# Projection chunks moved into the first stage, and an output projection that is summed in PSUM by column blocks

## The chip, the cores and the metric

The kernel runs on one core of a Trainium2 chip. The metric is the device time of one execution in microseconds (us), as the median of several runs. A trace of one execution was taken with the hardware profiler. TensorE is called PE (its weight loads PEld), VectorE is DVE, ScalarE is ACT, GpSimd is POOL, and SyncE, which issues the large loads, is SP.

## What is computed

One layer of a transformer encoder over 256 tokens of width 2048, in f32, with modulation vectors computed from a condition vector `c`:

```python
mod = silu(c) @ mod_w + mod_b                       # 2048 -> 6 x 2048
sh_m, sc_m, g_m, sh_f, sc_f, g_f = split(mod, 6)
h = x * (1 + sc_m) + sh_m
q, k, v = split(h @ w_qkv + b_qkv)                  # 32 query heads, 8 key/value heads of 64
o = windowed_attention(rope(q), rope(k), v, sink)   # |q - k| <= 128, a sink logit per head
y = o @ w_o + b_o
x = layer_norm(alpha * x + (1 + g_m) * y)
h = x * (1 + sc_f) + sh_f
y = relu(h @ w1 + b1) ** 2 @ w2 + b2                # 2048 -> 8192 -> 2048
x = layer_norm(alpha * x + (1 + g_f) * y)
```

## The kernel before

**Weights.** All matrices come as chunks of 128 x 2048 f32 (1 MB), loaded by SP into five raw buffers, and three more in the first stage. To keep f32 accuracy, ACT casts each half of a chunk to a rounded high part (`wh`, lines 382 and 393), and DVE subtracts it from the raw half to get the low part (`wl`, line 351). Five high and five low halves may be ready ahead. A product is three matmuls (`mm3`, lines 685 to 687): high x high, high x low, low x high, each with 512 output columns. A chunk of the projection to queries, keys and values (24 chunks) or of the output projection (16) is 24 such matmuls; half a chunk is 12.

**The stream.** `S.plan` lists every chunk in the order of use. `S.pump` walks this list strictly in order: it issues loads while a buffer is free, casts and splits halves while there is room, and hands modulation chunks to their own step. `S.main` pumps until the next chunk has both halves ready, `S.done` after each half. `S.pace` is the number of modulation chunks that one call may take on the way.

**Modulation.** 96 chunks of `mod_w` are vector times matrix. A chunk is taken either by PE, with the condition vector as the weights (line 458, a "row" chunk), or by DVE, which multiplies the chunk with the broadcast vector and sums along each row (line 498, a "column" chunk). `MIXP` says for each of the 16 groups of the mixer whether PE takes it, `FFP` how many of the four columns of a feed-forward group go to PE, `GMP` how many blocks of the mixer's gate.

**First stage** (0 to about 143 us). `SEQ` is the order of loading: entry `n` is a chunk with four units (one k-tile of 128 rows times 512 columns) of three column blocks that are summed in six PSUM banks over all 16 k-tiles; entry `(g, p)` is a chunk with four k-tiles of another column block, whose two token tiles share one bank in turn, and each is added to SBUF when done (`quarter`, line 784); the list behind an entry names the modulation groups loaded after it. `first_order()` (line 80) writes out the order of the instructions of the three engines with a planner's costs and due times, and these are pinned. The other seven chunks of this projection are in `LATE`.

**Attention and output projection.** The loop from line 1121 runs 21 slots. Slots 0 to 15 each do the scores of half a head group and a token tile (line 922), the maximum on DVE (line 929), the exponential on ACT (line 939), and in the next slot the transposes (line 964) with their copies (line 966); the values (line 980) come every second slot and give `oT[j]` for one of four head groups `j`. Each slot also takes one whole chunk: LATE chunks up to slot 4, then output-projection chunks `(c, j)` (column block `c`, head group `j`) in the order of `OUTS`, all `c` for one `j` before the next. `project` (line 1034) takes two new PSUM banks for each chunk, and DVE then adds them to an SBUF tile `y` (lines 1075 and 1077); at `j == 2`, `project_0` (lines 1088, 1089) multiplies `y` by the gate and adds it to the scaled residual; at `j == 3`, `add_gated` (lines 989 to 991) adds the last part and gathers the statistics of the norm. The bias comes by a broadcast over all partitions. `SLOT_FILL` says how many modulation chunks are planned before each slot's chunk, first the gate's, then those of the feed-forward groups. The order on each engine is mostly program order; the framework's scheduler may move an instruction that is ready ahead of one that waits. After the loop come the norm, the first feed-forward matrix (from line 1221), and the rest.

## Time and profile before

| | |
|---|---|
| median of 3 runs | 1085.61 us (1085.3 to 1085.9) |
| span of the profiled execution | 1083.7 us, 1.9 us under that median |
| PE busy | 1064.7 us (98% of the span) |
| DVE busy | 785.3 us (72%) |
| ACT busy | 527.5 us (49%) |
| read from HBM | 289.57 MB |

The profiled execution has no time of its own beside its span; the 1.9 us that lie around the span are the difference to the median of the runs. Busy shares are averages over stages with different limits. Overlapping matmuls count as busy throughout, so PE's share says little of its gaps; the distance from the start of one matmul to the next says more.

### The profile page before, as it was taken

To read this page: it belongs to the slowest core of one execution; us is meant where nothing else is said; L and a number is where in the kernel's file an instruction comes from. 1 tells how busy PE (TensorE), PEld (TensorE's weight loads), DVE (VectorE), ACT (ScalarE), POOL (GpSimd) and SP (SyncE) were. 2 spreads that over 40 slices of the span, in tenths; PEclk is the share of its full clock that TensorE was granted. 3 is DMA by queue.
4 is the path that set the end of the run, shared out by engine and by line. 5 is a ranking of instruction groups with operands and counts; after the bars stand their busy time and mean duration, and the time that the engine had idled before them with its cause. 6 is when DMAs were issued, how large, how long until landed. Compare 5 with 4: busy or idle time off the path is not lost.

```text
span 1083.7 us, 16256 instructions
## 1 busy us (share of the span) xinstructions
PE 1064.7 (98%) x6519; PEld 881.5 (81%) x6519; DVE 785.3 (72%) x1134; ACT 527.5 (49%) x814; POOL 19.7 (2%) x41
## 2 busy tenths in 40 slices
PE   8999999999999999999999999999999999999997
PEld 6777776677777899988888888888888888888885
DVE  3587689798799888754688789656665557665795
ACT  2453348777772646633345443344553334554340
POOL 2000000000000000000000010000000000000000
PEclk9999999999999999999999999999999999999999
DMA  9999997898973997555777889756555555557522
GB/s 380 425 425 425 427 407 270 352 348 344 391 277 122 420 352 273 193 194 194 272 272 274 295 293 319 297 203 222 194 194 188 192 193 201 181 181 263 194 78 78
DMA packets 43692, 292.75 MB, mean 270 GB/s; under 512 B 4916, under 2 KB 5076, under 8 KB 9824
## 3 DMA queue, kind: packets, MB, share of 16 engines
q1 hardware_dynamic: 40256, 281.82, 69.3%
q0 software_dynamic: 2496, 8.43, 2.3%
q10 hardware_dynamic: 864, 1.45, 0.4%
q8 instruction: 51, 0.84, 0.3%
q14 instruction: 25, 0.20, 0.0%
HBM read 289.57 MB, written 2.11 MB: 269 GB/s over the span
## 4 chain that ended last, share of the span: by engine, by line
PE 91%; DVE 5%; DMA 1%; ACT 1%; issue 1%; SPq 0%; DVEq 0%; ACTq 0%
PE pa L685 17%; PE pa L687 17%; PE pa L686 16%; PE pa L1264 16%; PE pa L1266 8%; PE pa L1240 3%; PE pa L1238 3%; PE pa L1239 3%; DVE raw L498 2%; PE pm L458 2%; PE gv L458 1%; PE pa L922 1%; PE pt L964 1%; PE pa L980 1%; DMA raw<-in_mod 1%; DVE wl L351 1%
## 5 line engine op out<-in xcount | busy, mean ns | idle before, releaser
L351 DVE TENSOR_TENSOR wl<-raw,wh 128x1024 fp32r<-128x1024 f32 x332 | 403.7, 1222 | 222.4 <-ACT wh L382 205.6
L382 ACT CAST wh<-raw 128x1024 fp32r<-128x1024 f32 x298 | 311.6, 1052 | 346.3 <-PE pa L687 203.1
L685 PE MATMUL pa<-wh,g 128*128 128x512 f32 x816 | 324.1, 398 | 2.7 <-ACT g L782 1.4
L687 PE MATMUL pa<-wh,g 128*128 128x512 f32 x816 | 319.3, 391 | 0.5 <-DVE g L984 0.4
L686 PE MATMUL pa<-wl,g 128*128 128x512 f32 x816 | 319.0, 391 | 0.5 <-DVE wl L351 0.4
L1264 PE MATMUL pa<-g,wh 128*128 128x512 f32 x768 | 192.3, 392 | 0.0
L685 PEld LDWEIGHTS pa<-wh,g 128*128 128x128 f32 x816 | 153.3, 188 | 42.7 <-issue 8.2
L687 PEld LDWEIGHTS pa<-wh,g 128*128 128x128 f32 x816 | 153.3, 188 | 34.6 <-issue 1.3
L686 PEld LDWEIGHTS pa<-wl,g 128*128 128x128 f32 x816 | 153.5, 188 | 31.4 <-DVE wl L351 1.2
L1264 PEld LDWEIGHTS pa<-g,wh 128*128 128x128 f32 x768 | 138.3, 189 | 25.1 <-ACT wh L382 0.2
L498 DVE CUSTOM_DVE_ANT_0 raw<-raw,cb 128x2048 f32<-128x2048 f32 x52 | 118.5, 2283 | 9.3 <-ACT cb L868 5.6
L1266 PEld LDWEIGHTS pa<-g,wl 128*128 128x128 f32 x768 | 104.8, 190 | 7.5
L1266 PE MATMUL pa<-g,wl 128*128 128x256 f32 x768 | 107.1, 282 | 0.0
L1240 PE MATMUL pa<-g,wl 128*128 128x256 f32 x256 | 72.3, 284 | 1.9 <-DVE wl L351 1.9
L1238 PE MATMUL pa<-g,wh 128*128 128x256 f32 x256 | 72.7, 285 | 0.3 <-ACT g L1173 0.3
L1239 PE MATMUL pa<-g,wh 128*128 128x256 f32 x256 | 72.4, 284 | 0.0
L1240 PEld LDWEIGHTS pa<-g,wl 128*128 128x128 f32 x256 | 48.9, 192 | 2.1 <-DVE wl L351 2.1
L1238 PEld LDWEIGHTS pa<-g,wh 128*128 128x128 f32 x256 | 49.1, 192 | 1.0 <-ACT g L1173 0.6
L1239 PEld LDWEIGHTS pa<-g,wh 128*128 128x128 f32 x256 | 49.1, 192 | 0.4 <-issue 0.4
L393 ACT CAST wh<-raw 128x1024 fp32r<-128x1024 f32 x34 | 34.8, 1048 | 21.8 <-DMA raw<-in_wqkv 19.6
L939 ACT ACTIVATE g<-g,nm 128x256 f32<-128x256 f32 x64 | 31.8, 498 | 13.1 <-DVE nm L929 13.0
L929 DVE CUSTOM_DVE_ANT_0 g<-pa,msk,nsnk 128x256 f32<-128x256 f32 x64 | 27.1, 477 | 6.3 <-PE pa L922 6.3
(204 smaller groups left out, 743.6 us busy)
## 6 DMA issues: line engine op xcount, KB each, us to landing
raw<-in_mod SPq DMA_DIRECT2D x96, 1024.0 KB, 8.8
raw<-in_w SPq DMA_DIRECT2D x64, 1024.0 KB, 4.8
raw<-in_w1b SPq DMA_DIRECT2D x48, 1024.0 KB, 4.8
raw<-in_wqkv SPq DMA_DIRECT2D x24, 1024.0 KB, 15.3
raw<-in_wo SPq DMA_DIRECT2D x16, 1024.0 KB, 7.4
raw<-in_w1a SPq DMA_DIRECT2D x16, 1024.0 KB, 7.4
g<-in_x SPq DMA_DIRECT2D x4, 512.0 KB, 9.1
gb<-in_lnrow POOLq DMA_DIRECT2D x8, 256.0 KB, 5.7
```

The lines of the kernel that those rows point to most:

```text
L351: self.pinned(nc.vector.tensor_sub(l, r, f32(self.hs[n])))
L382: self.last[n] = nc.scalar.copy(h, s)
L393: self.pinned(nc.scalar.copy(h, s))
L498: S.pinned(nc.vector.tensor_tensor_reduce(out=raw, in0=raw, in1=cb, scale=1.0, scalar=0.0, op0=OP.mult, op1=OP.add, accum_out=self.dst))
L685: S.pinned(nc.tensor.matmul(ps, xh, wh, start=start, stop=False))
L686: nc.tensor.matmul(ps, xh, wl, start=False, stop=False)
L687: S.prev = nc.tensor.matmul(ps, xl, wh, start=False, stop=stop).ins
L1238: nc.tensor.matmul(o, wh(w, 128), hh, start=new, stop=False)
L1239: nc.tensor.matmul(o, wh(w, 128), hl, start=False, stop=False)
L1240: nc.tensor.matmul(o, wl(w, 128), hh, start=False, stop=end)
L1264: nc.tensor.matmul(ps, wh(k, 128), ff_in(k), start=k == 0, stop=False)
L1266: nc.tensor.matmul(ps[:, :256], wl(k, 128), ff_in(k)[:, :256], start=False, stop=k == NK - 1)
```

## The change

In the first stage, four more chunks of the projection are taken as quarters, 21 of 24 in all, in a new order (`SEQ`), and `LATE` shrinks to three. DVE takes seven mixer groups instead of six, and all of feed-forward groups 0 and 1; PE takes 12 chunks of the mixer's gate instead of 8, in three blocks of 512 columns instead of one of 1024.

The output projection sums a column block in two PSUM banks over all four head groups, with the bias added by a matmul (from a row loaded in slot 2 and split in slot 3), so that nothing is added on DVE until the block is whole; then `add_gated` also scales the residual. `OUTS` alternates column blocks 0 and 1 beside the attention and takes blocks 2 and 3 after it. `HALVES` says how many halves of a chunk each slot takes, starting with the two chunks ahead of slot 0: slots 0 and 1 one half, 2 to 4 none (they pump twice), 5 to 16 one, 17 to 26 two. There are 27 slots, the pace is 1 in them, and the gate is spread in slot 15 instead of 11.

```diff
-OUT_AT = 5
-X_AT = 11
-SLOT_FILL = (1, 1, 1, 1, 1, 1, 1, 2, 2, 2, 2, 2, 2, 2, 2, 2, 2, 2, 2, 2, 1, 0, 0)
+HALVES = (2, 2, 1, 1, 0, 0, 0, 1, 1, 1, 1, 1, 1, 1, 1, 1, 1, 1, 1, 2, 2, 2, 2, 2, 2, 2, 2, 2, 2)
+X_AT = 12
+SLOT_FILL = (2, 2, 2, 3, 3, 3, 1, 0, 0, 1, 0, 0, 1, 0, 0, 1, 0, 0, 1, 2, 2, 2, 2, 2, 2, 1, 1, 0, 0)
 MIXG = (1,) * 16
-MIXP = tuple(int(k not in (4, 6, 8, 10, 12, 14)) for k in range(16))
+MIXP = tuple(int(k not in (6, 7, 9, 11, 12, 13, 15)) for k in range(16))
 FFG = (4, 4, 4, 4)
-FFP = (2, 2, 4, 0)
-GMP = 1
+FFP = (0, 0, 4, 0)
+GMP = 3
...
-        out += [("rg" + which, h, i, 0) for h in range(p) for i in range(8)]
-        out += [("cg" + which, 0, k, 0) for k in range(8 * p, NK)]
+        out += [("rg" + which, h, i, 0) for h in range(p) for i in range(4)]
+        out += [("cg" + which, 0, k, 0) for k in range(4 * p, NK)]
...
-SEQ = [(0, [1, 2]), (1, [3]), (2, []), ((0, 3), [4]), ((0, 4), [5]), (3, [6]), (4, [7]), (5, []), ((1, 3), [8]), ((1, 4), [9]), (6, [10]), (7, [11]), (8, [12]), ((2, 3), [13]), (9, [14]), (10, [15]), (11, [])]
+SEQ = [(0, []), (1, [1, 2, 3]), (2, []), ((0, 5), []), ((0, 3), []), (3, [4, 5, 6]), ((0, 4), []), (4, [7]), ((1, 4), []), (5, []), ((1, 5), [8]), (6, [9]), ((1, 3), []), (7, [10, 11]), ((2, 5), []), (8, [12]), ((2, 3), []), (9, [13]), ((2, 4), [14]), (10, []), (11, [15])]
...
-        def add(ps, c):
-            nc.tensor.matmul(ps, sel[:, c * 128:c * 128 + 128], hl, start=False, stop=True)
+        def add(ps, c, stop=True):
+            nc.tensor.matmul(ps, sel[:, c * 128:c * 128 + 128], hl, start=False, stop=stop)
...
-                m = Mod([MODS["rg" + which, h, i, 0] for i in range(8)], 256)
+                m = Mod([MODS["rg" + which, h, i, 0] for i in range(4)], 128)
...
-            nc.scalar.copy(r, m.ps[:, :256])
-            for x in range(2):
-                nc.tensor.transpose(pt[:, x * 128:x * 128 + 128], r[:, x * 128:x * 128 + 128], ident)
-            v = pt[:, :256].rearrange("p (x j q) -> p j x q", x=2, j=4)[:, :, :, 0]
-            d = self.col[:, 8 * h:8 * h + 8].rearrange("p (j x) -> p j x", j=4)
-            b = self.gb[:, 8 * h:8 * h + 8].rearrange("p (j x) -> p j x", j=4)
+            nc.scalar.copy(r[:, :128], m.ps[:, :128])
+            nc.tensor.transpose(pt[:, :128], r[:, :128], ident)
+            v = pt[:, :128].rearrange("p (j q) -> p j q", j=4)[:, :, 0]
+            d, b = (u[:, 4 * h:4 * h + 4] for u in (self.col, self.gb))
             nc.vector.tensor_tensor(d, v, b, op=OP.add)
...
-    LATE = [(3, 3), (2, 4), (3, 4), (0, 5), (1, 5), (2, 5), (3, 5)]
+    LATE = [(3, 3), (3, 4), (3, 5)]
...
-    OUTS = [(c, j) for j in range(4) for c in range(4)]
-    for n in range(-PRE, OUT_AT + 16):
+    OUTS = [(0, 0), (1, 0), (0, 1), (1, 1), (0, 2), (1, 2), (0, 3), (1, 3), (2, 0), (2, 1), (2, 2), (2, 3), (3, 0), (3, 1), (3, 2), (3, 3)]
+    halves = taken = 0
+    for n in range(-PRE, len(HALVES) - PRE):
         plan_late(SLOT_FILL[n + PRE])
         if n == X_AT:
             S.side[len(S.q)] = lambda: load_rows()
-        if n + PRE < len(LATE):
-            wq(*LATE[n + PRE])
-        elif n >= OUT_AT:
-            S.plan(a["wo"][OUTS[n - OUT_AT]])
+        halves += HALVES[n + PRE]
+        while 2 * taken < halves:
+            v = (LATE + OUTS)[taken]
+            if taken < len(LATE):
+                wq(*v)
+            else:
+                S.plan(a["wo"][v])
+            taken += 1
...
-    BEGIN = [(3, 3), (2, 4), (0, 5)]
+    BEGIN = [(3, 3), (3, 4), (3, 5)]
...
-    def add_gated(ps, t, c, gt, stats):
+    def add_gated(ps, t, c, gt, stats, scale=None):
         tmp = sml.tile([128, 512], F32, name="tmp", tag="t2", bufs=3)
         z = part(xs, t, c)
         nc.vector.tensor_tensor(tmp, ps, gt(c), op=OP.mult)
-        nc.vector.tensor_add(z, z, tmp)
+        if scale is None:
+            nc.vector.tensor_add(z, z, tmp)
+        else:
+            nc.vector.scalar_tensor_tensor(z, z, scale, tmp, op0=OP.mult, op1=OP.add)
         nc.vector.bn_stats(stats[t][:, c], z)
...
+    out_of = {}
+
     def project(c, j):
 
-        pss = [bank() for _ in range(NT)]
...
-                mm3(pss[t], oh[:, s], ol[:, s], wh(r), wl(r), r == 0, r == 3)
+                mm3(pss[t], oh[:, s], ol[:, s], wh(r), wl(r), j == 0 and r == 0, j == 3 and r == 3)
...
+                add_gated(pss[t], t, c, g1, st, ALPHA)
...
         for r in (0, 2):
             for t in range(NT):
                 step(t, (r, r + 1))
+            if r and j == 0:
+                for t in range(NT):
+                    bo(pss[t], c, False)
             S.done()
             if r == 0:
                 yield
-        for t, ps in enumerate(pss):
-            if j == 0 and t == 0:
-                ys[c] = g4b()
-            y = part(ys, t, c)
-            if j == 0:
-                nc.vector.tensor_add(y, ps, bo(c))
-            elif j < 3:
-                nc.vector.tensor_add(y, y, ps)
-            else:
-                add_gated(ps, t, c, g1, st)
-        if j == 2:
-            project_0(c)
-
-
-    def project_0(c):
-
-        for t in range(NT):
-            y, z = part(ys, t, c), part(xs, t, c)
-            nc.vector.tensor_mul(y, y, g1(c))
-            nc.vector.scalar_tensor_tensor(z, z, ALPHA, y, op0=OP.mult, op1=OP.add)
+        if j == 3:
+            for t in range(NT):
+                add_gated(pss[t], t, c, g1, st, ALPHA)
...
+    def chain():
+        for v in LATE[PRE:]:
+            yield from qkv(*v)
+            yield
+        for v in OUTS:
+            yield from project(*v)
+            yield
+
     todo = []
+    work = chain()
     S.behind = True
-    for n in range(OUT_AT + 16):
+    S.pace = 1
+    for n in range(len(HALVES) - PRE):
...
+        k = HALVES[n + PRE]
...
-        next(w, None)
+        if k:
+            next(work)
+        else:
+            S.pump(2)
         for f in mid:
             f()
-        next(w, None)
+        if k > 1:
+            next(work)
         if 0 < n <= 16 and n % 2 == 0:
             todo.append(values(n - 1))
-        if n == 11:
+        if n == 2:
+            split_bo, bo = bias_rows(a["bo"], D)
+        if n == 3:
+            split_bo()
+        if n == 15:
             g1 = m_gm.spread([g4(), g4()])
             st = [sml.tile([128, 4, 6], F32, name=f"st{t}", bufs=2) for t in range(NT)]
-        if n == 17:
+        if n == 24:
             ff_columns(0)
+    S.pace = VECS
```

More of the change, by code (lines that the diff above doesn't have):

```diff
@@ L571, in __init__ @@
             for h in range(p):
-                m = Mod([MODS["rg" + which, h, i, 0] for i in range(8)], 256)
+                m = Mod([MODS["rg" + which, h, i, 0] for i in range(4)], 128)
                 m.out = lambda m=m, h=h: self.rows(m, h)
                 self.ms.append(m)
-                rows += [(m, i) for i in range(8)]
+                rows += [(m, i) for i in range(4)]
             self.col = cst.tile([128, NK], F32, name="col" + which)
             cols = [(Col(MODS["cg" + which, 0, k, 0], self.col[:, k:k + 1]), 0)
-                    for k in range(8 * p, NK)]
+                    for k in range(4 * p, NK)]
             self.set(rows, cols)
@@ L1032, in normed @@
             tc.keep_in_program_order(nc.vector.tensor_scalar(z, z, mv[:, 0:1], rstd, op0=OP.subtract, op1=OP.mult))
+    out_of = {}
     def project(c, j):
-        pss = [bank() for _ in range(NT)]
+        pss = out_of[c] = out_of.get(c) or banks()
         last = j == 3 and c == 3
```

12 lines of the change are left out of this document (2 added, 10 removed).

## The prediction, made before the change was run

> **What bounds the kernel now.** I read the page first, then the busy time by stage, then the groups of the attention stage, then single instructions. From the page: busy engines, granted clock, and the chain that ended last.
>
> ```profile
> PE 1064.7 (98%) x6519; PEld 881.5 (81%) x6519; DVE 785.3 (72%) x1134; ACT 527.5 (49%) x814; POOL 19.7 (2%) x41
> ...
> PEclk9999999999999999999999999999999999999999
> ...
> PE 91%; DVE 5%; DMA 1%; ACT 1%; issue 1%; SPq 0%; DVEq 0%; ACTq 0%
> ```
>
> PE carries 91% of the chain at a full clock: time is PE's work plus PE's gaps. Busy time by stretch (PE, PEld, DVE, ACT, POOL, clock, DMA share, GB/s):
>
> ```profile
> 0.00:143.50 143.50, 134.94 (x1129) 105.36 (x1129) 90.47 (x137) 55.83 (x79) 6.19 (x18) 0.99 1.00 417
> 143.50:165.00 21.50, 21.10 (x133) 15.25 (x131) 20.48 (x23) 8.81 (x13) 0.64 (x2) 1.00 0.86 358
> 165.00:325.50 160.50, 159.75 (x1162) 115.92 (x1161) 140.24 (x302) 122.33 (x297) 3.15 (x6) 1.00 0.88 335
> 325.50:349.50 24.00, 24.00 (x117) 19.06 (x117) 21.72 (x37) 4.96 (x6) 0.00 (x0) 1.00 0.36 128
> 349.50:405.00 55.50, 51.85 (x476) 48.13 (x476) 47.50 (x77) 32.86 (x49) 0.00 (x0) 1.00 0.95 369
> 405.00:1083.70 678.70, 673.09 (x3514) 577.74 (x3513) 464.89 (x562) 302.73 (x373) 9.74 (x16) 1.00 0.62 218
> ```
>
> These are the first stage, the way into the attention, the 16 attention slots, the end of the output projection, the start of the feed-forward, and the rest. The change ends at 349.5, so I keep the last two rows as they are. PE's busy time hides its gaps, since matmuls overlap; two neighbours from the timeline and four entries of the chain give the real price of one:
>
> ```profile
> 346.67 0.39 PE L685 MATMUL pa<-wh,g 128*128 128x512 f32 x1
> 346.89 0.39 PE L686 MATMUL pa<-wl,g 128*128 128x512 f32 x1
> 347.12 0.39 PE L687 MATMUL pa<-wh,g 128*128 128x512 f32 x1
> ```
> ```profile
> 131.39 1.01 PE gv L458 x32
> ...
> 188.87 1.88 PE pa L980 x16
> 190.74 1.06 PE pa L922 x8
> ...
> 224.31 1.02 PE pt L964 x8
> ```
>
> A matmul of 512 columns costs 0.227 us from start to start ((347.12-346.67)/2, with the rounding), so a weight chunk of 24 costs 5.45 and half a chunk 2.72. A modulation chunk on PE costs 1.01. An attention slot costs scores 1.06, transposes 1.02 and half of a values step of 1.88: 3.02. In 165 to 325.5 that is 16 x 3.02 = 48.3, three rounds of query transposes (8 of the L964 kind each) 3.1, and, by the two rows below, 131 x 3 matmuls = 89.2 and modulation 16.1: together 156.7 of 160.5, or 97.6%. PE's gaps there are 3.8.
>
> ```profile
> 165.00:325.50 160.50, 52.09 (x131) 24.58 (x131) 1.00 0.88 335
> ...
> 165.00:325.50 160.50, 16.13 (x368) 9.41 (x368) 1.00 0.88 335
> ```
>
> These are the same stretch for line 687 alone, then for line 458 alone.
>
> **PE's work.** Modulation moves from PE to DVE: the mixer's groups lose one (2 chunks), feed-forward groups 0 and 1 lose 4 each, the mixer's gate gains 4 (12 instead of 8): 6 fewer, -6.1 us. The output bias, until now added by DVE, becomes 8 matmuls of 512 columns: +1.8. Transposes for the gate rise by one and for the others fall by two: nothing. Sum **-4.2**.
>
> **First stage.** Four more weight chunks come here and leave the later stages: 4 x 5.45 = 21.8 us of PE, moved. This stage was 143.5 and becomes about 143.5+21.8-2.0 = 163.3. Its cover is data: up to 143.5 the queue moved 143.5 x 0.417 = 59.8 MB, while 49 loads and x are 53.5, so 4 more loads (4.2 MB, 10 us at that rate) arrive earlier than PE can use them. DVE has 90.5 there and gets 8 low halves, 2 columns and 6 evictions, priced from these rows:
>
> ```profile
> L351 DVE TENSOR_TENSOR wl<-raw,wh 128x1024 fp32r<-128x1024 f32 x35 | 42.5, 1219 | 20.1 <-ACT wh L393 15.1 <-ACT wh L382 5.0
> L498 DVE CUSTOM_DVE_ANT_0 raw<-raw,cb 128x2048 f32<-128x2048 f32 x12 | 27.2, 2284 | 5.6 <-ACT cb L868 5.6
> ...
> L784 DVE TENSOR_TENSOR g<-g,pa 128x512 f32<-128x512 f32 x6 | 4.1, 686 | 6.6 <-PE pa L687 6.5
> ...
> ACT wh L393 <- DMA raw<-in_wqkv: 18.6, 5, 4.4
> ```
>
> 8 x 1.22 + 2 x 2.28 + 6 x 0.69 = 18.5: 109 of 163, not a bound. The last row (waits, 27 to 143) says that the cast waited 18.6 us in sum for weights to land; the new order asks for weights ahead of several modulation pairs. PE is idle 8.6 (143.5-134.94) in this stage, a part of it before the first data, where nothing is altered. I take **-2**; bounds -4 (about half of that idle gone) and +3 (nine quarter chunks instead of five share one bank, each with an eviction of 0.69 that the next must await; other units cover it now).
>
> **Attention.** Up to now a slot carried a whole chunk, 5.45 of PE. Now slots 0 and 1 carry half each, 2 to 4 none, 5 to 15 half each, because only two column blocks may be open and each needs the head group just finished. DVE, the second-busiest, is relieved (groups of 165 to 325):
>
> ```profile
> L1077 DVE TENSOR_TENSOR g4b<-g4b,pa 128x512 f32<-128x512 f32 x15 | 10.2, 681 | 3.5 <-PE pa L687 3.5
> L1075 DVE TENSOR_TENSOR g4b<-pa,g4b 128x512 f32<-128x512 f32 x8 | 5.4, 685 | 1.7 <-PE pa L687 1.7
> ...
> L1088 DVE TENSOR_TENSOR g4b<-g4b,g 128x512 f32<-128x512 f32 x7 | 4.6, 682 | 0.0
> L1089 DVE SCALAR_TENSOR_TENSOR g<-g,g4b 128x512 f32<-128x512 f32 x6 | 3.9, 684 | 0.0
> ```
>
> These 24.1 us go. DVE was not the bound, so by themselves they bring nothing. ACT becomes the tightest (groups, then one slot in order of time):
>
> ```profile
> L382 ACT CAST wh<-raw 128x1024 fp32r<-128x1024 f32 x34 | 35.4, 1043 | 13.0 <-PE pa L687 12.7
> L939 ACT ACTIVATE g<-g,nm 128x256 f32<-128x256 f32 x64 | 31.8, 498 | 13.1 <-DVE nm L929 13.0
> L954 ACT ACTIVATE g<-g,rs 128x256 f32<-128x256 f32 x64 | 27.6, 501 | 5.5 <-DVE rs L951 5.2
> L966 ACT COPY g<-pt 128x512 f32<-128x512 f32 x32 | 17.1, 576 | 2.4 <-PE pt L964 2.4
> ```
> ```profile
> 234.70 0.19 ACT L941 ACTIVATE es<-es 128x4 f32<-128x4 f32 x1
> 234.94 1.04 ACT L382 CAST wh<-raw 128x1024 fp32r<-128x1024 f32 x1
> 235.89 1.71 ACT L954 ACTIVATE g<-g,rs 128x256 f32<-128x256 f32 x4
> ```
>
> Only the casts shrink with the chunks: 122.3-35.4 = 86.9 stays, and 13 halves (2 of the last projection chunk, 11 of the output projection) add 13.5: 100.4. PE has 48.3+3.1+13 x 2.72+9 gate chunks 9.1+4 bias matmuls 0.9 = 96.8. ACT is now the longer lane. If it reaches the 97.6% that PE reached, the stage takes 102.9, PE's gaps are 6.1 instead of 3.8, and this costs **+2.3**. Bounds: -3.8 (PE is fed from elsewhere and loses nothing) and +12.6, the slower case below.
>
> A rule speaks against thinner slots. The Trainium skill, TensorE: Matmul & The Clock Gate, section What's actually happening, says that TensorE falls to half its clock after an idle window of about 3.4 us. By it each such gap would cost another 1.7 us as an estimate. The trace agrees as far as it goes: the granted clock is 1.00 from 143.5 on, where PE's gaps are small, and below that only at the start, as the rival on the clock quotes.
>
> **After the attention.** Ten chunks follow, 20 x 2.72 = 54.4 of PE. DVE gets some 20 low halves (24.4), 10 to 12 columns (23 to 27) and 6 gated additions of three passes each:
>
> ```profile
> L989 DVE TENSOR_TENSOR tmp<-pa,g 128x512 f32<-128x512 f32 x7 | 4.8, 686 | 2.1 <-PE pa L687 2.0
> L991 DVE BATCH_NORM_STATS2 st<-g 128x6 f32<-128x512 f32 x7 | 4.7, 687 | 0.1
> L990 DVE TENSOR_TENSOR g<-g,tmp 128x512 f32<-128x512 f32 x7 | 4.7, 683 | 0.1
> ```
>
> 6 x 2.06 = 12.3, so 60 to 64 against 54.4. Five low halves made ahead are 13.6 us of PE's work and cover that debt; bounds 0 and +5, I take **+1**. The gate row is now spread after slot 15 and first used in slot 18. Its way through memory (timeline of POOL, then the DMA issues with their us to landing):
>
> ```profile
> 281.41 0.51 POOL L600 DMA_DIRECT2D rowm<-grow  x1 [12.74 <-ACT grow L599]
> 286.82 1.08 POOL L602 DMA_DIRECT2D g<-rowm  x2 [4.91 <-DMA rowm<-grow]
> ```
> ```profile
> g<-rowm POOLq DMA_DIRECT2D x2, 512.0 KB, 11.6
> ```
>
> From the write's issue at 281.41 to 286.82+11.6 = 298.4 are 17 us, against two to three slots of 5.5 to 8. It may come a little late; then DVE stands at the first gated addition with the low halves queued behind it, and the same five halves cover PE. Nothing taken. The new addition with a scale (0.684 at line 1089) costs what the plain one does (0.683 at line 990). Splitting the bias is a few operations in slots 2 and 3, where DVE has room, and the 1 MB of bias broadcast goes away.
>
> **Sum.** -4.2-2+2.3+1 = -2.9. The profiled span of 1083.7 becomes 1080.8; the median of the runs stands 1.9 above the span (1085.6-1083.7), so the forecast is **1082.7 us**.
>
> **Rivals.**
> *PE alone sets the pace.* The order of the instructions may let PE take halves early whenever ACT is behind. Then the gaps beside the attention are gone (-3.8), the first stage gains 3, and the tail costs nothing: 1085.6-4.2-3.8-3 = 1074.6; with a little lost, 1076. For it: PE reached 97.6% in the old stage. Against it: ACT's own lane of 100.4 is longer than PE's 96.8.
>
> *ACT's latency, slower.* In a slot with half a chunk nothing lies between the transposes and the values step, so PE stands until ACT has copied both transposed tiles, and scores follow only then. ACT per two slots: exponentials 2.2 (4 x 0.5 and 0.19), cast 0.95, copies 1.07, scaling 1.7, all twice, and one cast of the result 0.58: 12.4; and it stands about 1.5 in every second slot, since the values step and the next scores (1.88+1.06) outlast the scaling (1.7): 13.9 for two, 6.95 each. Without a chunk, 5.95 each. 11 x 6.95 + 5 x 5.95 = 106.2, the first output chunk has nothing made ahead (+2), and the way from scores 15 to values 15 is bare (+5): 113.2, gaps 16.4 instead of 3.8, +12.6. With nothing won in the first stage and 2.5 lost at the end: 1085.6-4.2+12.6+2.5 = 1096.5. It decides as soon as a slot takes over 6.7 us on average. For it: ACT waited 13.0 on DVE's maxima at line 939 even with slack. Against it: the scores of the next slot depend on none of this and can go first.
>
> *The clock falls.* At the start, where PE waits for the first data, the granted clock was lower (same columns as the stretches above):
>
> ```profile
> 0.00:27.00 27.00, 22.61 (x244) 16.33 (x244) 9.12 (x31) 6.57 (x11) 6.19 (x18) 0.94 0.94 380
> ```
>
> 0.06 x 27 = 1.6 us of PE's work lost. Were that to happen in slots 2 to 4 and once at the end of the attention, on top of the slower case: 1096.5+4 x 1.6 = 1103. Against it: gaps there should be under 2 us, and the old stage's gaps left the clock at 1.00. The skill's rule cited above is this mechanism.
>
> *It cancels.* Four banks held from slot 5 on leave four for scores (2), transposes and values; the moved work and the lost cover balance: 1085.6.
>
> **How the numbers follow.** Forecast case 0.50, its own range 1078 to 1090; PE alone 0.22; ACT's latency 0.22; the clock 0.02; cancelled 0.04. No change means within 0.2%, 2.2 us, about what a measurement can tell. Of the forecast's half, 0.22 lies below 1083.4, 0.17 within, 0.11 above. Faster 0.22+0.22 = 0.44, same 0.17+0.04 = 0.21, slower 0.11+0.24 = 0.35. The range 1073 to 1098 takes in the bounds of the attention term.
>
> **What will show it.** The last bias matmul of the first stage should end near 163, not before 143.5 as now; if it ends after 167, the first-stage step is wrong. From first scores to the last values step should be about 103; over 110 means the latency case, under 98 the first rival. ACT should be busy over 90% of that stretch. Tail matmuls should run 0.227 apart, else DVE's debt was not covered. Line 458 should show 38 chunks' worth (6 fewer) and line 498 58 columns. The forecast fails if slots 5 to 15 show PE waiting over 1 us each for line 966's copies or for casts, or if anything after 405 moves.

## The result, and the profile after

The changed kernel takes 1113.89 us (median of 4 runs, 1111.92 to 1116.54); the kernel before, beside it, 1085.76 us. The ratio is 1.0259, 95% interval 1.0241 to 1.0278: slower by 28 us, above the predicted range of 1073 to 1098. The profiled execution has a span of 1114.8 us against 1083.7. Every ratio here and below is of fast runs and leaves out one execution, the profiled one of the last kernel, which took 3724.6 us.

From the page of the kernel after: busy engines, and the granted clock in 40 slices.

```profile
PE 1076.5 (97%) x6460; PEld 890.0 (80%) x6460; DVE 782.6 (70%) x1116; ACT 528.7 (47%) x814; POOL 22.4 (2%) x45
...
PEclk9999999889999999999999999999999999999999
```

Every busy share is about what it was. Only the two eights in the clock's line say where to look. Busy time by stretch of the kernel after (PE, PEld, DVE, ACT, POOL, clock, DMA share, GB/s): first stage, way in, slots 0 to 4, slots 5 to 14, slot 15 to the last values, tail, start of the feed-forward, rest.

```profile
0.00:158.40 158.40, 151.90 (x1159) 120.89 (x1159) 110.85 (x159) 64.81 (x87) 6.21 (x18) 1.00 1.00 417
158.40:190.90 32.50, 25.20 (x330) 18.79 (x328) 24.62 (x30) 8.51 (x14) 1.14 (x2) 0.95 0.91 345
190.90:234.30 43.40, 30.01 (x259) 19.16 (x260) 34.41 (x81) 29.09 (x75) 3.68 (x6) 0.82 0.86 328
234.30:304.80 70.50, 70.43 (x382) 48.44 (x381) 56.48 (x151) 62.12 (x175) 0.00 (x0) 0.99 0.58 201
304.80:323.50 18.70, 18.70 (x95) 13.06 (x95) 13.27 (x26) 12.20 (x29) 1.63 (x3) 1.00 0.78 279
323.50:379.00 55.50, 53.81 (x259) 42.39 (x255) 31.57 (x39) 16.28 (x16) 0.00 (x0) 1.00 0.61 222
379.00:434.50 55.50, 51.85 (x470) 48.03 (x470) 47.08 (x73) 33.10 (x49) 0.00 (x0) 0.99 0.94 368
434.50:1114.80 680.30, 674.65 (x3519) 579.29 (x3517) 464.36 (x562) 302.65 (x373) 9.77 (x16) 1.00 0.62 218
```

The same columns of the kernel before, for slots 0 to 4 and 5 to 14 (cut at the first scores and at the scores of slots 5 and 15):

```profile
165.10:209.50 44.40, 44.13 (x285) 31.00 (x285) 36.06 (x82) 37.65 (x91) 0.40 (x1) 1.00 0.86 320
209.50:310.40 100.90, 100.43 (x792) 73.29 (x790) 89.77 (x193) 72.83 (x181) 2.64 (x5) 1.00 0.94 359
```

Slots 0 to 4 hold 24 matmuls on weights now, where they held 103, and four modulation chunks as before (128 narrow matmuls for 64 wide ones): almost half of PE's work there is gone. They take 43.4 us, where they took 44.4. To see this in each stage I count PE's instructions and price them from start to start as the prediction did: "work" is that sum, "gap" is the length less the work. For slots 0 to 4 of the kernel after these are the main groups (line, engine, operation, names, shapes and count, then busy time, mean ns and idle time before):

```profile
L983 PE MATMUL pa<-g,g 128*64 128x256 f32 x24 | 6.6, 571 | 0.0
L967 PE MATMUL pt<-ident,g 128*128 128x128 f32 x32 | 6.1, 320 | 2.7 <-ACT g L957 2.7
L925 PE MATMUL pa<-g,g 64*128 64x256 f32 x40 | 5.9, 412 | 0.2 <-ACT g L911 0.2
L458 PE MATMUL pm<-raw,cact 128*32 128x128 f32 x128 | 4.3, 276 | 0.0
L688 PE MATMUL pa<-wh,g 128*128 128x512 f32 x8 | 3.4, 420 | 0.0
```

24 x 1.88/16 + 32 x 1.02/8 + 40 x 1.06/8 + 128/32 x 1.01 + 3 x 8 x 0.227 = 21.7; with the query transposes and the bias matmuls 23.3. So 20.1 of 43.4 us are gap, and PE's 30 us of "busy" hold matmuls that took longer at the low clock (a matmul of line 983 took 571 ns on average here and 385 before). What the low clock adds is in the gap too.

| stage | before: length, gap | after: length, gap |
|---|---|---|
| first stage | 143.4, 18.4 | 158.4, 13.8 |
| way in | 21.7, 1.2 | 32.5, 10.1 |
| slots 0 to 4 | 44.4, 1.9 | 43.4, 20.1 |
| slots 5 to 14 | 100.9, 3.6 | 70.5, 10.1 |
| slot 15 to last values | 16.7, -0.1 | 18.7, 2.5 |
| tail | 22.0, 0.2 | 55.2, 2.7 |
| start of feed-forward | 56.0, 4.0 | 56.0, 4.7 |

Over the whole kernel work fell by 4.3 us, as predicted (4.2); by the table it is 5.2 in these stages, since a few matmuls more fall into the rest now (3519 against 3514). Gaps rose from 29.2 to 64.0, that is by 34.8, and 34.8-4.3 = 30.5 of the 31.1 us between the spans is told by that. Over half of the rise is in slots 0 to 4 (18.2), a quarter on the way in (8.9). PE's two longest waits in the kernel after between 158 and 240 (engine, tile and line, what it waited for: sum, times, longest):

```profile
PE pt L910 <- DVE rs L954: 10.3, 1, 10.3
...
PE pm L458 <- DMA raw<-in_mod: 6.2, 3, 3.7
```

The second is the way in: gate chunks that are not loaded yet stand in PE's line ahead of the query transposes. The first stands in slot 2; DVE's timeline there (start, length, engine, line, operation), then PE's:

```profile
203.69 2.15 DVE L889 TENSOR_TENSOR g<-g,trig 128x512 f32<-128x512 f32 x2
205.76 1.82 DVE L892 TENSOR_TENSOR g<-g,trig 128x512 f32<-128x512 f32 x2
...
209.32 1.22 DVE L351 TENSOR_TENSOR wl<-raw,wh 128x1024 fp32r<-128x1024 f32 x1
210.46 2.28 DVE L498 CUSTOM_DVE_ANT_0 raw<-raw,cb 128x2048 f32<-128x2048 f32 x1
...
212.67 3.49 DVE L351 TENSOR_TENSOR wl<-raw,wh 128x1024 fp32r<-128x1024 f32 x3
216.08 0.15 DVE L950 TENSOR_TENSOR rs<-sm,es 128x4 f32<-128x4 f32 x1
216.15 1.22 DVE L894 TENSOR_TENSOR g<-g,g 128x1024 f32<-128x1024 f32 x1
```
```profile
206.20 1.04 PE L967 MATMUL pt<-ident,g 128*128 128x128 f32 x8
217.51 1.94 PE L910 MATMUL pt<-ident,g 128*128 128x128 f32 x8 [10.28 <-DVE rs L954]
```

Four low halves and one column, 7.0 us in sum, are work for later chunks. They stand in DVE's line ahead of the softmax's small step (L950) and of the last addition of the rotary step (L894), for which the query transposes wait. PE has nothing else to do, since the slot has no chunk.

The gap of slots 5 to 14 is of another kind. The profile lists no wait of PE there. What grew is the scores (line 922 before, 925 after; groups of these slots, then PE's timeline in the kernel after):

```profile
L922 PE MATMUL pa<-g,g 64*128 64x256 f32 x82 | 11.8, 404 | 0.0
```
```profile
L925 PE MATMUL pa<-g,g 64*128 64x256 f32 x81 | 18.5, 421 | 0.0
```
```profile
280.63 1.13 PE L925 MATMUL pa<-g,g 64*128 64x256 f32 x8
281.69 0.50 PE L688 MATMUL pa<-wh,g 128*128 128x512 f32 x1
...
290.26 1.13 PE L925 MATMUL pa<-g,g 64*128 64x256 f32 x4
291.31 1.08 PE L983 MATMUL pa<-g,g 128*64 128x256 f32 x8
```

Eight score matmuls in one run hold PE for 1.06 us (281.69-280.63), the price used above; four alone hold it for 1.05, and the other four, after the values, for as long again. About as many matmuls are busy 6.7 us longer (18.5-11.8), and the gap of these slots rose by 6.5 (10.1-3.6). So here PE does not stand: the scores cost twice as much where the scheduler takes them apart. Why it does so is not shown.

### The profile page after: what moved, and what is told of

It reads as the page before. It is cut to its first block, busy times and chain, and to the rows that moved or that the text cites. A ratio compares the mean times of both kernels' runs of the same rounds, so it can differ in the third digit from the quotient of the medians.

```text
span 1114.8 us, 16139 instructions
## 1 busy us (share of the span) xinstructions
PE 1076.5 (97%) x6460; PEld 890.0 (80%) x6460; DVE 782.6 (70%) x1116; ACT 528.7 (47%) x814; POOL 22.4 (2%) x45
## 4 chain that ended last, share of the span: by engine, by line
PE 91%; DVE 4%; DMA 3%; ACT 1%; issue 1%; SPq 0%; DVEq 0%; ACTq 0%
PE pa L688 17%; PE pa L690 17%; PE pa L689 16%; PE pa L1271 16%; PE pa L1273 8%; PE pa L1245 3%; PE pa L1247 3%; PE pa L1246 3%; DMA raw<-in_mod 2%; PE pa L925 2%; PE pa L983 2%; PE gv L458 1%; PE pt L967 1%; PE pm L458 1%; DVE raw L498 1%
## 5 line engine op out<-in xcount | busy, mean ns | idle before, releaser
L1271 PE MATMUL pa<-g,wh 128*128 128x512 f32 x768 | 192.3, 392 | 0.0
L689 PEld LDWEIGHTS pa<-wl,g 128*128 128x128 f32 x816 | 153.4, 188 | 31.6 <-issue 0.7
L498 DVE CUSTOM_DVE_ANT_0 raw<-raw,cb 128x2048 f32<-128x2048 f32 x58 | 132.4, 2284 | 13.4 <-DMA raw<-in_mod 13.4
L932 DVE CUSTOM_DVE_ANT_0 g<-pa,msk,nsnk 128x256 f32<-128x256 f32 x64 | 27.9, 479 | 13.2 <-PE pa L925 13.0
L942 ACT ACTIVATE g<-g,nm 128x256 f32<-128x256 f32 x64 | 31.8, 500 | 4.7 <-DVE nm L932 4.6
```

The costliest lines, as they stand in the source:

```text
L498: S.pinned(nc.vector.tensor_tensor_reduce(out=raw, in0=raw, in1=cb, scale=1.0, scalar=0.0, op0=OP.mult, op1=OP.add, accum_out=self.dst))
L689: nc.tensor.matmul(ps, xh, wl, start=False, stop=False)
L1271: nc.tensor.matmul(ps, wh(k, 128), ff_in(k), start=k == 0, stop=False)
```

## The experiments

The theory formed on this, A in the texts below: work of the stream, put in the engines' lines ahead of the attention's own chain, stretches the slots that were emptied. B stands for the rival that each text names.

**The pumps of the empty slots.** Each of slots 2 to 4 calls `S.pump(2)`: it is one call, which may take up to two modulation chunks. First moved behind the slot's own steps, then left out:

```diff
-        else:
-            S.pump(2)
         for f in mid:
             f()
+        if not k:
+            S.pump(2)      # in the second kernel these two lines are absent
```

> In slots 2 to 4, which carry no half chunk, the changed kernel takes work from the stream (two modulation chunks, casts and low halves) ahead of the rotary step's last addition and of the query transposes; here the stream is called after them. Theory A (the 10.3 us that PE waits before the query transposes of slot 2 come from low halves and columns standing ahead of the rotary addition on DVE): that wait falls under 2 us, the half-clock stretch behind it goes, and the kernel becomes 8 to 12 us faster than the changed one, near 1104. Theory B (the slots are too thin, and PE waits for the chain anyway): the wait moves to another instruction of the same slots, and the time stays within 3 us of 1114.

> The changed kernel, where slots 2 to 4 take nothing from the stream at all (no modulation chunk, no cast, no low half). Theory A (the stream's work on DVE and ACT in these slots is what stretches them): slots 0 to 5 fall from 43.4 us to 34 or less, of which slot 5 gives a part back, and the kernel becomes 3 to 8 us faster. Theory B (a slot without a chunk takes about 8 us by the chain from scores to values itself): slots 0 to 5 stay above 40 us, the stream's work comes late in slot 5, and the kernel becomes 3 to 8 us slower, 1117 to 1122.

Moved, 1111.62 us (ratio to before 1.024, 1.0221 to 1.0258), only 2.3 less, and the intervals of the two kernels overlap. The wait was not gone, it had moved. DVE and PE of the kernel with the moved pumps, one slot later:

```profile
211.79 4.60 DVE L351 TENSOR_TENSOR wl<-raw,wh 128x1024 fp32r<-128x1024 f32 x4
216.31 2.29 DVE L498 CUSTOM_DVE_ANT_0 raw<-raw,cb 128x2048 f32<-128x2048 f32 x1
...
218.52 1.29 DVE L889 TENSOR_TENSOR g4b<-g,trig 128x512 f32<-128x512 f32 x2
...
222.19 0.48 DVE L932 CUSTOM_DVE_ANT_0 g<-pa,msk,nsnk 128x256 f32<-128x256 f32 x1
```
```profile
226.42 1.94 PE L967 MATMUL pt<-ident,g 128*128 128x128 f32 x7 [9.56 <-ACT g L957]
```

The end of one slot is the beginning of the next: now the same passes, and a rotary step behind them, stand ahead of the next softmax (L932). Left out, 1100.64 us (1.0131, 1.011 to 1.0152), 13.3 less. Slots 0 to 4 of that kernel:

```profile
189.10:221.10 32.00, 26.08 (x258) 17.42 (x258) 24.82 (x71) 29.07 (x79) 4.21 (x7) 1.00 0.93 372
```

Same matmuls (258), 11.4 us shorter, with DVE busy 24.8 in place of 34.4. So the pumps cost 13 us; this is shown. The clock is whole here too, which this run alone does not tell apart.

**The clock.** 84 and 20 transposes of the identity, which nothing uses, in slots 2 and 3, to give PE something to do while it waits:

```diff
+    def fill(n):
+        ps = bank()
+        for _ in range(n):
+            nc.tensor.transpose(ps[:, :128], ident, ident)
...
+            if n in (2, 3):
+                mid.append(lambda: fill(84 if n == 2 else 20))
```

> The changed kernel with idle transposes of a constant added on PE where it stood still: 84 (about 9 us) ahead of the query transposes of slot 2 and 20 (about 2 us) ahead of the next scores. They compute nothing that is used. Theory A (the two half-clock stretches of 10.2 and 6.8 us behind these gaps cost time of their own): the clock stays whole from 207 to 240 us, slots 2 to 5 become 3 to 5 us shorter, and the kernel lands near 1110. Theory B (the slots are set by ACT and DVE, so a slower PE costs nothing there): the clock is whole and the time stays within 1.5 us of 1113.9.

1117.63 us (1.0284, 1.0258 to 1.0311). Slots 0 to 4:

```profile
190.00:233.00 43.00, 39.28 (x362) 29.22 (x361) 34.02 (x81) 29.11 (x76) 3.67 (x6) 0.93 0.88 338
```

The first half-clock stretch went and the second stayed, so the clock rose from 0.82 to 0.93 and not to 1. The slots did not get shorter, with 43.0 against 43.4: the slow PE of slot 2 costs nothing that this shows. The intervals of the two kernels overlap; in the profiled executions what is lost against the changed kernel comes in the tail, where DVE waited 7.6 us for the gate row instead of 4.2.

**Where the modulation chunks stand.** One chunk in each slot instead of 2 and 3 in the early ones; then the same with the pumps moved behind:

```diff
-SLOT_FILL = (2, 2, 2, 3, 3, 3, 1, 0, 0, 1, 0, 0, 1, 0, 0, 1, 0, 0, 1, 2, 2, 2, 2, 2, 2, 1, 1, 0, 0)
+SLOT_FILL = (1,) * 19 + (2,) * 6 + (1, 1, 1, 0)
```

> Only the number of modulation chunks planned before each slot's chunk is changed: one in each of the first 19 slots, two in six, then three times one, instead of 2,2,2,3,3,3 at the front and nearly none after. Theory A (PE's waits before slot 0 come from gate chunks that are loaded one after another at 2.6 us each with only five buffers, and stand in PE's queue ahead of the query transposes): the way from the end of the first stage to the first scores falls from 32 us to 23 or less, PE's waits for modulation loads go from 6.2 us to under 1, and the kernel becomes about 8 us faster, near 1106. Theory B (those waits only fill time that the transposes would have needed anyway, since DVE's rotary steps set the first scores): the first scores stay near 190 us and the time stays within 3 us of 1114.

> Both single edits together: modulation spread evenly over the slots, and the stream called after the rotary step and the query transposes in slots 2 to 4. If the two remove different waits, their gains (6.3 and 2.3 us) add: 1105.3. If flat modulation already took away what stood ahead of the rotary step: 1107.5, no more than it alone. Neither theory expects less than 1100: slots 0 to 5 carry only 21 us of PE work, and half chunks stay in slots 5 to 15.

1107.55 us (1.0199, 1.0183 to 1.0215) and 1108.2 (1.0204, 1.0186 to 1.0221). Slots 0 to 4 fell to 31.9 us, as without pumps. The way in kept a gap of 9.0, slots 5 to 9 rose by 2.4 us, and the tail grew by 4.8, where DVE now waited 7.1 us for the gate row and PE 4.0 behind it (1.7 in the changed kernel). With fewer passes to bring forward, where the pumps stand makes no difference.

**The parts alone.** The new order of the first stage on the kernel before, with pumps in the four slots that it empties (`SEQ` and `BEGIN` are those of the change too):

```diff
-    LATE = [(3, 3), (2, 4), (3, 4), (0, 5), (1, 5), (2, 5), (3, 5)]
+    LATE = [(3, 3), (3, 4), (3, 5)]
...
+        if 1 <= n < OUT_AT:
+            S.pump(2)
```

> The kernel before with only the first stage changed: the new loading order with 21 of 24 projection chunks and three late ones; the output projection, the modulation split and whole chunks per slot stay as before. Slots 1 to 4 then carry no chunk (they take two modulation chunks each). Theory A (moving chunks forward is free in the first stage, and what it costs is the cover that slots 1 to 4 lose): the first stage ends near 161, slots 0 to 4 take 30 to 36 us instead of 44 while 21.8 us of work have left them, so the kernel is 8 to 14 us slower than before, 1094 to 1100. Theory B (the loss comes from the output projection alone): within 3 us of 1085.8.

1100.77 us (1.0134, 1.0117 to 1.0151). Slots 0 to 4:

```profile
180.70:222.20 41.50, 33.41 (x178) 19.56 (x178) 35.20 (x83) 28.57 (x79) 0.00 (x0) 0.75 0.75 283
```

PE's work in these slots fell by 20.3 us (42.4 to 22.1), and they shrank by 2.9, from 44.4 to 41.5: the work moved was a cover. What lies below it here holds the pumps too; without pumps the same slots of the changed kernel took 32.0. The first stage itself did what was hoped (gap 14.7, not 18.4).

The modulation's split alone (`MIXP`, `FFP`, `GMP` and the gate in blocks of 512, as in the change):

```diff
-MIXP = tuple(int(k not in (4, 6, 8, 10, 12, 14)) for k in range(16))
-FFP = (2, 2, 4, 0)
-GMP = 1
+MIXP = tuple(int(k not in (6, 7, 9, 11, 12, 13, 15)) for k in range(16))
+FFP = (0, 0, 4, 0)
+GMP = 3
```

> The kernel before with only the new split of the modulation between PE and DVE: seven mixer groups on DVE instead of six, all of feed-forward groups 0 and 1 on DVE, 12 gate chunks on PE instead of 8. First stage, late chunks and output projection as before. Theory A (PE alone sets the time, so 6 chunks fewer on it at 1.01 us are worth 6 us): 1079 to 1081, faster than both. Theory B (DVE, busy 140 of 160 us in the attention, becomes late with 6 more columns of 2.28 us): PE's gaps grow by as much, and the time stays between 1084 and 1092.

1091.12 us (1.0047, 1.0029 to 1.0065). PE takes 38 modulation chunks instead of 44, 6.1 us less, and the kernel loses 5. In slot 10 two columns stand ahead of a rotary addition on DVE, and PE waits (waits between 255 and 280):

```profile
PE pt L905 <- DVE g4b L889: 5.2, 1, 5.2
```

The half clock follows (a mean of 0.83 from 260.5 to 279.0), and this slot takes 18.4 us, where it took 11.5. No run took this one wait away.

Column blocks with the first stage of before, first with the gate row's last step after slot 15, then after slot 11:

```diff
-SEQ, LATE, BEGIN as in the change
+SEQ, LATE, BEGIN as before
-HALVES = (2, 2, 1, 1, 0, 0, 0, ...
+HALVES = (2, 2, 2, 2, 2, 2, 2, ...
+SLOT_FILL = (1,) * 19 + (2,) * 6 + (1, 1, 1, 0)
...
-        if n == 15:      # only in the second kernel
+        if n == 11:
```

> The changed kernel with the first stage and the seven late chunks of before: whole late chunks in slots up to 4, one half of an output chunk in slots 5 to 16, two halves after; output projection in PSUM and the modulation split as changed, modulation spread evenly. Theory A (the loss sits in the way into the attention and in slots 0 to 4, which are full again here): gaps only in slots 5 to 15, about 1 us each, against 4 us of PE work saved: 1085 to 1093. Theory B (half chunks beside the attention are what costs, in every slot): slots 5 to 15 take over 7.5 us each, and the kernel lands above 1097.

> The column-block kernel with the first stage of before, and the gate row's last step after slot 11 in place of slot 15. Theory A (the 7.2 us wait for the gate row at the first low part of the tail is on the path): TensorE's gap of the tail falls from 6.6 to about 1 us, and the time from 1096 to 1089 to 1091. Theory B (what comes free there is waited for elsewhere, or the POOL work and the row's transfer disturb an earlier slot): 1094 to 1098 us.

1096.04 us (1.0094, 1.0078 to 1.011) and 1090.65 (1.0045, 1.0027 to 1.0063). The tail with the late row, its wait, and the tail with the early row:

```profile
298.60:358.70 60.10, 56.01 (x261) 44.29 (x259) 38.99 (x48) 16.39 (x16) 0.00 (x0) 0.97 0.66 250
```
```profile
DVE tmp L992 <- DMA g<-rowm: 7.2, 1, 7.2
```
```profile
303.40:355.20 51.80, 51.80 (x252) 41.24 (x249) 34.39 (x42) 16.42 (x16) 0.00 (x0) 1.00 0.71 264
```

The late row was on the path, for 5.4 us. With it early, column blocks and the modulation's split stand at 1.0045, and the split alone at 1.0047: the column blocks bring and cost nothing that can be told.

**What sets a slot of 7 us.** On that kernel, each slot's normalise, rotary step and transposes go ahead of its chunk steps; or the low halves of weights beside the attention and in the first blocks of the tail are left out (the high half is used a second time in their place, so there are as many matmuls):

```diff
-        if k:
-            next(work)
-        else:
-            S.pump(2)
         for f in mid:
             f()
-        if k > 1:
-            next(work)
+        for _ in range(k):
+            next(work)
```
```diff
-            l = (g4, g4b)[kept - 1](F32R) if kept else wlp.tile([128, 1024], F32R, name="wl")
-            self.pinned(nc.vector.tensor_sub(l, r, f32(self.hs[n])))
+            if self.behind:
+                l = self.hs[n]
+            else:
+                l = (g4, g4b)[kept - 1](F32R) if kept else wlp.tile([128, 1024], F32R, name="wl")
+                self.pinned(nc.vector.tensor_sub(l, r, f32(self.hs[n])))
```

> The kernel outproj_gate with each slot's normalise, rotary step and transposes put ahead of the slot's column-block or late-chunk steps in the program. Theory A (in slots 5 to 14 the passes on VectorE and ScalarE that stand ahead of the softmax set the 7.0 us of a slot): slots at 6.3 to 6.6 us, 4 to 7 us below outproj_gate. Theory B (the softmax chain's own latency sets them, or the scheduler has put the chain first already): within 1.5 us of outproj_gate. Third: the probabilities' transposes come up before their normalisation is done, and TensorE stands: more than 2 us above outproj_gate.

> The kernel outproj_gate in which the low halves of weights streamed beside the attention and in the tail's first blocks are not formed; their products use the high half a second time, so TensorE's work is the same, ScalarE's too, and VectorE has 1.2 us less for every half chunk (this leaves out the correction of the weights there). Theory A (VectorE's load and order set a slot): slots 5 to 14 go from 7.0 to 6.2 to 6.5 us, 5 to 8 us below outproj_gate in all. Theory B (ScalarE's chain sets it): slots stay at 6.9 to 7.1 us, within 2 us of outproj_gate.

1100.71 us (1.0135, 1.0114 to 1.0156), 10 more: the third case, with slots 0 to 4 at 51.6 instead of 44.0 (PE waits 5.5 us there for the scaling that the transposes need) and slots 5 to 14 at 75.3 instead of 71.5. And 1088.58 (1.0018, 1.0006 to 1.0029), 2.1 less. Slots 5 to 14 of the kernel with all low halves, then without:

```profile
211.30:282.80 71.50, 71.36 (x513) 50.53 (x511) 62.37 (x155) 58.68 (x165) 1.59 (x3) 1.00 0.87 326
```
```profile
209.70:279.80 70.10, 69.96 (x508) 50.02 (x506) 52.48 (x145) 58.23 (x162) 1.59 (x3) 1.00 0.87 326
```

DVE lost 9.9 us of work and the ten slots 1.4. DVE's load is not what holds a slot at 7.0 us. ACT is the same in both, but that does not leave ACT's chain as the cause: neither profile lists a wait of PE in these slots, and PE's priced work is about 66 of the 71.5 us. So the 6.2 to 6.5 us a slot that the expectation named could not be reached, and as far as the profile shows PE's own line holds these slots.

**The other edits, and all together.** One modulation chunk at a time ahead of the two late chunks; the gate row after slot 11 in the changed kernel; both without the pumps; and the first of them without the pumps:

```diff
-    S.pace = VECS
+    S.pace = 1
```

> The changed kernel with one edit: the pace is one modulation chunk per call already for the two late chunks ahead of slot 0, instead of two. Theory A (on the way into the attention PE's gap of 10.1 us comes from gate chunks that the stream takes too early, so that they stand in PE's queue, not yet loaded, ahead of the query transposes): the gap falls under 4 us, the first scores come before 185 us instead of 190.9, and the kernel becomes 4 to 8 us faster, 1106 to 1110. Theory B (the chunks are late because only five buffers serve 19 loads in a row, in whatever order PE takes them): first scores stay at 189 to 191 and the time within 2 us of 1113.9.

> The changed kernel with one edit: the gate row is spread after slot 11 instead of slot 15. Its chunks are all taken by slot 5. Theory A (after the last values step DVE waits 4.2 us for the broadcast gate row, and the low half of that step's result stands behind this wait, so PE stops too): that wait goes, PE's gap after the attention falls from 2.7 to about 1 us, and the kernel becomes 1 to 4 us faster. Theory B (the low halves that are ready cover it): no change within 1 us.

> Three edits on the changed kernel together: nothing taken from the stream in slots 2 to 4, pace 1 ahead of slot 0, gate row spread after slot 11. If the waits they remove are the loss: from 1100.6 (the first edit alone) down by 4 to 8 us for the way in, to 1093 to 1097. What is left over 1086 is then the cover that slots 0 to 4 and the half chunks lack: gaps of 6 to 9 us in slots 0 to 4 and 4 to 5 more than before in slots 5 to 15. If it reaches 1086 or less, empty slots cost nothing by themselves and the whole loss was order.

> The kernel without the extra pumps, and with one modulation chunk at a time ahead of the two late chunks; the gate row's last step stays after slot 15. Theory A (passes on VectorE and chunks on TensorE taken out of the way in are only put off into slots 5 to 9, where they stand ahead of the steps' softmax): 1102 to 1107 us, slots 5 to 9 about 46 us long as in the kernel with all three edits. Theory B (it was the gate row's earlier step that ate the gain of the three edits): 1089 to 1094 us, slots 5 to 9 at 33 to 37 us.

1101.57 us (1.0144, 1.0129 to 1.0159), 12.3 less and more than expected: first scores came at 178.3, not 190.9, and the gain stayed to the last values (311.2, not 323.5). Four of the eight gate chunks of the way in moved into slots 0 to 4, which took 42.2 us all the same. 1113.61 us (1.0252, 1.0235 to 1.027) for the gate row alone: nothing, though its wait is gone from the profile. All three: 1105.01 (1.0176, 1.016 to 1.0191), worse than two of its parts. Pumps and pace without the gate row: 1108.95 (1.0212, 1.0194 to 1.023). So it is these two that don't add, and the early gate row, worth nothing alone, is worth 3.9 here. Slots 5 to 9 of the kernel without pumps and with pace 1:

```profile
212.70:258.40 45.70, 40.94 (x321) 28.82 (x320) 34.63 (x80) 35.08 (x88) 0.00 (x0) 0.91 0.78 304
```

They take 45.7 us, against 35.1 in the changed kernel. 128 modulation matmuls and 9 low halves fall in these slots, where the kernel that only lacks the pumps has none and 4. The kernel with all three edits has the same 128 and 9 there, and shows what they do, on DVE, then on PE:

```profile
227.63 4.80 DVE L351 TENSOR_TENSOR wl<-raw,wh 128x1024 fp32r<-128x1024 f32 x4 [1.31 <-ACT wh L382]
232.35 2.29 DVE L498 CUSTOM_DVE_ANT_0 raw<-raw,cb 128x2048 f32<-128x2048 f32 x1
...
234.56 0.48 DVE L932 CUSTOM_DVE_ANT_0 g<-pa,msk,nsnk 128x256 f32<-128x256 f32 x1
```
```profile
235.91 1.55 PE L983 MATMUL pa<-g,g 128*64 128x256 f32 x6 [3.25 <-DVE nm L932]
```

The chunks that neither the way in nor the pumps took are taken when the first output chunks need them, and again 7 us of passes stand ahead of a softmax, for which PE waits 3.3 us; the four chunks themselves are 4.0 us of PE's work. The debt was put off, not paid. The rest of the 10.6 us was not followed wait by wait.

**A version of before.** Two of the change's pieces on the kernel before: feed-forward columns and gate as in the change, pace 1 in the slots:

```diff
-FFP = (2, 2, 4, 0)
-GMP = 1
+FFP = (0, 0, 4, 0)
+GMP = 3
...
+    S.pace = 1
```

> The kernel before with feed-forward groups 0 and 1 all on DVE, 12 gate chunks on PE instead of 8, and a pace of one modulation chunk per call in the slots; the mixer's groups, the first stage and the output projection as before. PE loses 4 chunks, 4.0 us. Theory A (the full new split failed by pairs of columns standing ahead of the rotary step on DVE and by a first stage that gained nothing): 1081 to 1084, faster than both kernels. Theory B (DVE is too full for any more columns): 1086 or more.

1092.63 us (1.0062, 1.0045 to 1.0079): slower than before, as theory B has it, also with the mixer's groups as before and one chunk per call. No profile here shows where these 7 us are. No kernel run here beats the one before.

## Why the prediction was wrong

By ratios to before, the parts form a path: the modulation's split +5 us (1.0047), column blocks with an early gate row 0 (1.0045), the late gate row +5 (1.0094), the new first stage with its halves and fill +18 (1.0259). Each was summed near nothing.

- **PE's work, -4.2: right in size** (-4.3), wrong as a gain. Work that moves to DVE was credited in full. Alone the split cost 5 us; the one long wait read for it is columns on DVE in line ahead of the rotary step. The trap was "DVE was not the bound": it has room on average, but what counts is what stands ahead of one small instruction.
- **First stage, -2: right in kind, small in size.** It ended at 158.4, not 163.3; its gap fell by 4.6, past the bound of 4. Of the 4.9 us between, 2.2 are a mixer group less on PE, which stood in the term before.
- **Way in, taken as unchanged: wrong.** 32.5 us instead of 21.7. `SLOT_FILL` put more gate chunks there and the pace let them through together; they waited for their loads in PE's line. The attention's sum counted nine gate chunks; four fell there and eight on the way in. The edit of one number, the pace, brought 12.3 us.
- **Attention, +2.3: this step failed most.** It compared sums of the stage, ACT 100.4 and PE 96.8, and let the longer one be filled to 97.6%. First scores to last values took 323.5-190.9 = 132.6, not 103, with ACT busy 29.1+62.1+12.2 = 103.4 of it, or 78%. A slot is a chain, and its length is not in the sums: a slot of the first five cost 8.7 us with half a chunk or none, and 6.4 without pumps, where half a chunk is 2.72 of PE's work. Of the rise in gaps 18.2 is in these five: mostly waits of PE behind passes on DVE and ACT that the sum held to be covered, and the low clock after them. Another 6.5 is in slots 5 to 14, where the sum priced the scores of a slot at 1.06 and those taken apart cost about twice that.
- **The rival on ACT's latency named the right direction, and its numbers fit in part by luck.** It said 6.95 for a slot with half a chunk, measured 7.05 (70.5/10); and 2 x 6.95 + 3 x 5.95 = 31.8 for the first five, measured 32.0 without the pumps (its own sum counted all five as empty). In slots 5 to 14 the match is luck: PE does not stand there for ACT's copies or anything else, and the length comes from the scores. In the first five without pumps PE does wait 3.6 us for ACT's scaling and 2.3 for DVE, so a chain is there; that it is ACT's latency is argued, not shown. Its 1096.5 lacked the way in, the pumped passes and the split.
- **After the attention, +1 with the gate row at nothing: mis-sized.** The debt was not there: DVE is busy 31.6 us in the tail, not 60 to 64, with no column in it. The row was, and five halves made ahead did not cover it: 5.4 us where slots before run well. In the changed kernel the wait was 4.2, and removing it changed nothing measurable. The tail is otherwise near its work (gap 2.7).
- **The clock was the right event at the wrong price.** It fell in slots 2 and 4, which got 0.02 as a chance, behind waits of 10.3 and 2.7 us and not "under 2". Filling the first of them gained nothing, so the clock's own share of the loss is not shown.

What the prediction's tests said: 58 columns at line 498 and 38 chunks at line 458, as stated; the tail within 2.7 us of its work; the rest within 1.6 us (680.3 against 678.7). The stretch from first scores to last values, 132.6 us, was over the 110 that it named for the latency case. Its sign of failure, waits of over 1 us for copies or casts in slots 5 to 15, did not appear, although these slots failed: a profile need not list a wait where a stage grows.

The rule cited from the Trainium skill (TensorE: Matmul & The Clock Gate, section What's actually happening: half the clock after an idle window of about 3.4 us) agrees with this stretch of the kernel after, from the end of the transposes in slot 2:

```profile
207.30:211.40 4.10, 0.00 (x0) 0.00 (x0) 4.10 (x13) 3.38 (x11) 0.00 (x0) 1.00 0.58 232
211.50:221.70 10.20, 4.19 (x18) 2.75 (x20) 10.20 (x13) 5.15 (x10) 0.00 (x0) 0.50 0.78 268
```

PE idles 4.1 us at a full clock, then 0.50 is granted for 10.2 us, until about 4 us after PE's next work.

## What to carry to other kernels

Before moving big work out of a stage, find out what it covered: price the stage again as a chain of its small dependent steps, slot by slot, and not as sums per engine. Where an engine takes its work in order, read what stands ahead of each small instruction of that chain; work that prepares something later belongs behind it, and taking it away from one slot only helps if no later slot gets it back at a worse place. A price read from neighbouring instructions holds for that order; when a change moves them apart, read it again. Single edits that each remove a wait must be run together before their gains are added.

## What was not expected of the hardware

DVE's rotary multiplications took 2.15 and 1.82 us for two in slot 2 (rows above), 1.29 in other slots such as at 218.52 in the moved-pump kernel. At that moment POOL, idle in most slots, prepared the bias rows (timeline of POOL, kernel after):

```profile
203.21 0.95 POOL L279 MEMSET g<- 128x1024 f32 x1
...
204.64 0.65 POOL L283 TENSOR_SCALAR_AFFINE_SELECT g<-g 128x512 f32<-128x512 f32 x1
```

That is 0.86+0.53 = 1.4 us more on DVE. The Trainium skill, GPSIMD Engine Reference, section Key points, says that this engine shares its memory interfaces with VectorE and contends with instructions that read two inputs from SBUF; these rows agree. The record holds more of it. In the runs with early gate row, filled clock or moved pumps, POOL works in the same place and the two took 2.14 to 2.15 and 1.81 to 1.82. In the kernel without pumps POOL had done this work by 192.3, and the same two, from 201.88 on, took 1.28 and 1.29. Beside the fills with zeros alone (line 279; evenly spread modulation, from 184.60 on) a pair took 1.29 as well, which points to the selection of line 283.
